# Gate and up projections of the second channel mixer as seven block products of sums

## The chip, the cores and the metric

One core of a Trainium2 chip. The metric is the device time of one execution in microseconds, the median over the runs shown. The kernel is written in Bass with Tile: the program names tiles in pools, and a scheduler at build time sets the order of every engine's queue except TensorE's, which here runs in the order of the program.

## The reference, cut to what matters

The reference is one inference step of a two-layer backbone: 512 latent tokens and 128 context tokens, 640 in all, of width 1024. After the token mixers of each layer comes a SwiGLU channel mixer with a hidden width of 2816:

```python
def ffn_sublayer(x, mods, p):
    h = modulated_norm(x, p['norm2_g'], mods[3], mods[4])
    y = (jax.nn.silu(h @ p['ffn_w_gate']) * (h @ p['ffn_w_up'])) @ p['ffn_w_down']
    return x + mods[5] * y
```

All of it is in float32. The two projections `h @ ffn_w_gate` and `h @ ffn_w_up` of layer 1 (the second and last layer) are what the change rewrites.

## The kernel before, in words

The kernel keeps features on the partitions and the 640 tokens along the free axis. A float32 product runs on TensorE as three passes of the type float32r: each operand is split into a high part (a copy into float32r, on ScalarE, line 308) and a low part (source minus high part, on VectorE, line 309; both in `split`), and the passes are high by high, high by low, low by high. A pass over one 128 by 128 block of weights is a weight load and a matmul (`mm`, line 351).

The channel mixer stands in `run` (line 2070 and on). The hidden width is cut into 22 tiles of 128 features (index `f`), in three parts of 8, 7 and 7 tiles (`THIRDS`). For each tile, `fm_tile` loads a 128 by 1024 block of gate weights into a staging buffer (`weights`, tag `wst`, three buffers, one DMA of 512 KB on SyncE's queue, line 315), splits it into the tags `whi` and `wlo` (two buffers each), and runs 8 blocks of the contraction times 3 passes times 2 token halves: 48 matmuls, of 256 and of 384 columns (`SPLIT`). The same follows for the up weights. ScalarE takes the SiLU of the gate out of PSUM (line 2120), VectorE multiplies it by the up result (line 2128), and the product is split again (lines 308 and 309) into a tile `g` (tag `g`, 12 buffers). After a part, eight tiles of down weights (index `e`) multiply the part's `g` tiles, and `residual` (line 1810) adds the result to `x`. In the last part the down products run one token half after the other, so that the final norm can start early, and some of their split weights lie in buffers that `spare` finds.

Layer 1's first tiles differ: the gate and up of tile 0 and the gate of tile 1 run together by token halves (`by_halves`), because the normalised tokens `h` of the second half are still being made then (`norm_k`, whose low parts of odd blocks are made on GpSimd, line 584). `h` holds high and low parts of all 8 blocks of the width for 640 tokens. Nothing reads `h` after the last up projection of layer 1.

The accumulators are five PSUM banks handed out in turn. Nothing but the scheduler orders ScalarE, VectorE, GpSimd and the DMA queue among each other; a tile of a tag gets one of that tag's buffers when one is free, and its first writer waits until all readers of the buffer's last tile are done.

Of the kernel before, what the change touches and what calls it, by code (L numbers as in the profile page):

```python
# [11 lines left out]
F32 = mybir.dt.float32  # L12
F32R = mybir.dt.float32r
I32 = mybir.dt.int32
AF = mybir.ActivationFunctionType
ALU = mybir.AluOpType
# [4 lines left out]
D = 1024  # L21
KD = 8
NS = 512
NP = 128
T = NS + NP
HB = 256
SPLIT = (slice(0, HB), slice(HB, T))
L = 2
PAST = 256
FF = 2816  # L30
KF = FF // 128
# [256 lines left out]
class _Build:  # L288
# [35 lines left out]
    @staticmethod  # L324
    def spare(e, l, pool, n):

        tile = lambda shape, tag, bufs: pool.tile(shape, F32R, tag=tag, name="w2", bufs=bufs)
        if e < 2:
            ts = [tile([128, 2, T], "g", 12) for _ in range(2)]
        elif e == 3:  # L330
            t = tile([128, 2, D], "cb", 1)
            ts = [t[:, i] for i in range(2)]
        elif e in (4, 5):
            ts = [tile([128, D], *(("wmd", 2) if e == 4 else ("sg", 3))) for _ in range(2)]
        else:
            return None
        ts = [t.rearrange("p a n -> p (a n)") if len(t.shape) == 3 else t for t in ts]
        return [t[:, 0:128 * n].rearrange("p (k n) -> p k n", k=n) for t in ts]

    def put(self, oh, k, a, src, view=None):  # L340
# [334 lines left out]
    def half_steps(self, w, rhs, ks, h, acc, tag="fd"):  # L675

        od = self.od
        yield tag, 1
        o = self.half_tile(acc, tag, h)
        n = len(ks)  # L680
        for i, k in enumerate(ks):
            for c, (wt, part) in enumerate(((w[0], 0), (w[0], 1), (w[1], 0))):
                self.mm(o, wt[:, i, :], rhs(part, k)[:, SPLIT[h]], i == 0 and c == 0, i == n - 1 and c == 2)
            yield od.now
        return o

    def tm_chunk(self, srcs, h, n, pools, sink, room=None):

# [1381 lines left out]
    def run(self):  # L2070
        nc, A = self.nc, self.A
# [9 lines left out]
        h = hp.tile([128, 2, KD, T], F32R, tag="h", name="h", bufs=1)  # L2081
# [6 lines left out]
        ps = self.banks(P, W)  # L2088
        for l in range(L):
            hp, h, h_st, x, fx, fx_st, P, W = self.mixer(l, h, h_st, x, fx, fx_st, P, W, p_side, w_side)  # L2090
            p_side, w_side = w_side, p_side
            ps = self.banks(P, W)
            gpool, g_st = self.pool("g", side="left")
            for part, (f0, f1) in enumerate(THIRDS):
                g, kept = {}, {}
                last = lambda e, n=f1 - f0: self.weights(A["wd"][l, e, :, f0:f1], [128, n, 128],
                                                         parts=self.spare(e, l, gpool, n))
                for f in range(f0, f1):
                    if f == KF - 1:
                        kept.update((e, last(e)) for e in (0, 1))  # L2100
                    if f == 0:
                        r = []
                        parts = [gpool.tile([128, 2, T], F32R, tag="g", name="w2", bufs=12).rearrange("p a t -> p (a t)")
                                 [:, 0:D].rearrange("p (k n) -> p k n", k=KD) for _ in range(2)]
                        gen = self.by_halves([A["wg"][l, f], A["wu"][l, f]], lambda q, k, h=h: h[:, q, k], ps,
                                             more=(A["wg"][l, 1], parts))
# [8 lines left out]
                        og = og1  # L2115
                    else:
                        og = self.fm_tile(A["wg"][l, f], lambda q, k: h[:, q, k], range(KD), ps)
                    sg = gpool.tile([128, D], F32, tag="sg", name="sg", bufs=3)[:, :T]
                    for q in range(2):
                        nc.scalar.activation(sg[:, SPLIT[q]], og[q], AF.Silu)  # L2120
                    if f:
                        ou = self.fm_tile(A["wu"][l, f], lambda q, k: h[:, q, k], range(KD), ps)
                    if l + 1 < L:
                        self.modulate(f, gpool)
                    g[f - f0] = gt = gpool.tile([128, 2, T], F32R, tag="g", name="g", bufs=12)
                    for q in range(2):
                        s = SPLIT[q]
                        nc.vector.tensor_tensor(out=sg[:, s], in0=ou[q], in1=sg[:, s], op=ALU.mult)  # L2128
# [81 lines left out]
```

## Time and profile before

| | |
|---|---|
| three runs | 1956.04, 1961.34, 1962.57 us (median 1961.34) |
| the profiled execution | 1962.85 us, of which the span in the profile is 1961.0 us |
| mean granted TensorE clock | 0.978 of full speed |

The span runs from the first to the last instruction; the 1.85 us around it belong to the execution as well. In the rows further down times are microseconds from the start of the span, and a group of instructions is given by source line, engine, operation and the tiles it writes and reads. PE is TensorE's matmuls, PEld its weight loads (which overlap the matmuls), DVE is VectorE, ACT ScalarE, POOL GpSimd. A matmul's duration in these rows includes its way through the array; how many follow each other per microsecond is read from their start times.

### The profile page before, as it was taken

To read this page: it belongs to the slowest core of one execution; us is meant where nothing else is said; L and a number is where in the kernel's file an instruction comes from. 1 tells how busy PE (TensorE), PEld (TensorE's weight loads), DVE (VectorE), ACT (ScalarE), POOL (GpSimd) and SP (SyncE) were. 2 spreads that over 40 slices of the span, in tenths; PEclk is the share of its full clock that TensorE was granted. 3 is DMA by queue.
4 is the path that set the end of the run, shared out by engine and by line. 5 is a ranking of instruction groups with operands and counts; after the bars stand their busy time and mean duration, and the time that the engine had idled before them with its cause. 6 is when DMAs were issued, how large, how long until landed. Compare 5 with 4: busy or idle time off the path is not lost.

```text
span 1961.0 us, 40272 instructions
## 1 busy us (share of the span) xinstructions
PE 1847.3 (94%) x16620; PEld 1742.0 (89%) x16620; DVE 1070.1 (55%) x2304; ACT 727.5 (37%) x1497; POOL 329.7 (17%) x530
## 2 busy tenths in 40 slices
PE   5998998899999999999999999789999999999997
PEld 4986787778999999999998988678889999999997
DVE  6573546677557547647555854567655232233244
ACT  4632124766442112222346322367645221221231
POOL 1221521233300000000133271123322000000001
PEclk9997899999999999999999999899999999999999
DMA  7345423142445436436423322213342222222221
GB/s 299 122 119 135 125 78 104 31 110 79 139 138 172 140 108 193 150 109 189 133 91 101 98 66 67 77 44 84 95 151 65 76 76 76 76 68 83 75 97 54
DMA packets 114166, 210.35 MB, mean 107 GB/s; under 512 B 44160, under 2 KB 61312, under 8 KB 113856
## 3 DMA queue, kind: packets, MB, share of 16 engines
q1 hardware_dynamic: 105920, 202.74, 32.8%
q0 software_dynamic: 2816, 4.72, 1.2%
q8 instruction: 130, 2.13, 0.4%
q10 hardware_dynamic: 5248, 0.33, 0.2%
q14 instruction: 52, 0.43, 0.1%
HBM read 183.14 MB, written 19.89 MB: 104 GB/s over the span
## 4 chain that ended last, share of the span: by engine, by line
PE 78%; DVE 9%; ACT 5%; DMA 5%; issue 2%; POOL 1%; SPq 0%; DVEq 0%; ACTq 0%; POOLq 0%
PE acc L351 56%; PE tacc L351 6%; PE pvo L351 2%; PE ptp L363 2%; PE sc L351 2%; PE mpart L351 1%; PE invp L351 1%; DMA wst<-wout 1%; DVE wlo L309 1%; ACT p L1294 1%; ACT whi L308 1%; DMA wmd<-wmodT 1%; DMA wmd<-wmod 1%; ACT pt L1329 1%; PE ysp L351 1%
## 5 line engine op out<-in xcount | busy, mean ns | idle before, releaser
L351 PE MATMUL acc<-h,whi 128*128 128x256 f32 (+1 forms) x3520 | 679.0, 312 | 3.2 <-ACT h L574 1.4
L351 PEld LDWEIGHTS acc<-h,whi 128*128 128x128 f32 x3520 | 578.5, 189 | 11.7 <-issue 3.4
L308 ACT CAST whi<-wst 128x1024 fp32r<-128x1024 f32 (+3 forms) x202 | 196.9, 976 | 687.9 <-PE acc L351 645.0
L351 PE MATMUL acc<-h,wlo 128*128 128x256 f32 (+1 forms) x1760 | 411.1, 310 | 0.8 <-DVE wlo L309 0.8
L309 DVE TENSOR_TENSOR wlo<-wst,whi 128x1024 fp32r<-128x1024 f32 (+3 forms) x202 | 229.9, 1139 | 204.2 <-ACT whi L308 199.3
L351 PEld LDWEIGHTS acc<-h,wlo 128*128 128x128 f32 x1760 | 320.4, 189 | 2.5 <-DVE wlo L309 1.3
L351 PE MATMUL acc<-g,whi 128*128 128x256 f32 (+1 forms) x1128 | 216.7, 309 | 0.1
L541 POOL TENSOR_TENSOR sq<-sq 128x256 f32<-128x256 f32 (+1 forms) x48 | 45.4, 947 | 927.2 <-ACT sq L535 926.9
L1810 DVE SCALAR_TENSOR_TENSOR x<-acc,mods,x 128x256 f32<-128x256 f32 (+1 forms) x192 | 75.3, 434 | 210.6 <-PE acc L351 210.4
L351 PEld LDWEIGHTS acc<-g,whi 128*128 128x128 f32 x1128 | 185.9, 188 | 0.4 <-DVE g L309 0.4
L507 DVE SCALAR_TENSOR_TENSOR wmj<-wmd,cb 128x1024 f32<-128x1024 f32 x112 | 136.8, 1222 | 40.9 <-DMA wmd<-wmodT 39.6
L351 PE MATMUL tacc<-whi,h 128*128 128x256 f32 (+1 forms) x640 | 151.2, 317 | 1.0 <-ACT whi L308 0.8
L351 PE MATMUL acc<-g,wlo 128*128 128x384 f32 (+1 forms) x564 | 135.2, 309 | 0.0
L351 PEld LDWEIGHTS tacc<-whi,h 128*128 128x128 f32 x640 | 111.4, 194 | 11.8 <-issue 6.6
L351 PE MATMUL acc<-oh,whi 128*128 128x384 f32 (+1 forms) x512 | 114.6, 314 | 3.3 <-DVE xe L1810 1.9
L363 PE MATMUL ptp<-cbase,p 128*128 128x128 f32 x512 | 80.3, 283 | 27.8 <-ACT pt L1329 14.1
L351 PEld LDWEIGHTS acc<-g,wlo 128*128 128x128 f32 x564 | 103.2, 188 | 0.0
L351 PE MATMUL tacc<-wlo,h 128*128 128x256 f32 (+1 forms) x320 | 98.2, 307 | 1.3 <-DVE wlo L309 1.3
L363 PEld LDWEIGHTS ptp<-cbase,p 128*128 128x128 f32 x512 | 56.6, 141 | 43.9 <-ACT pt L1329 17.6
L2128 DVE TENSOR_TENSOR sg<-acc,sg 128x256 f32<-128x256 f32 x88 | 39.2, 485 | 101.9 <-PE acc L351 101.9
L1297 POOL TENSOR_SCALAR dg<-cbase,sd 128x128 f32<-128x128 f32 x96 | 58.8, 613 | 207.1 <-DVE sd L1295 150.0
L1294 ACT ACTIVATE p<-sc,sm 128x768 f32<-128x768 f32 (+1 forms) x96 | 79.8, 831 | 31.8 <-DVE sm L1291 23.6
(321 smaller groups left out, 2655.9 us busy)
## 6 DMA issues: line engine op xcount, KB each, us to landing
wmd<-wmodT SPq DMA_DIRECT2D x56, 512.0 KB
wst<-wg SPq DMA_DIRECT2D x44, 512.0 KB
wst<-wu SPq DMA_DIRECT2D x44, 512.0 KB
wmd<-wmod SPq DMA_DIRECT2D x40, 512.0 KB
wst<-wd SPq DMA_DIRECT2D x34, 448.0 KB
wst<-wfm SPq DMA_DIRECT2D x24, 512.0 KB
wst<-wd SPq DMA_DIRECT2D x16, 512.0 KB
wst<-wtma SPq DMA_DIRECT2D x12, 512.0 KB
```

What stands on the lines that cost most here:

```text
L308: self.nc.scalar.copy(hi, src)
L309: self.nc.vector.tensor_tensor(out=lo, in0=src, in1=hi.bitcast(F32), op=ALU.subtract)
L351: self.nc.tensor.matmul(out, lhsT, rhs, start=start, stop=stop)
L363: self.nc.tensor.transpose(out, in_, self.ident)
L507: nc.vector.scalar_tensor_tensor(out=j, in0=st, scalar=1.0, in1=self.cb[:, g], op0=ALU.mult, op1=ALU.mult, accum_out=self.msum[:, e, g:g + 1])
L541: (eng or nc.gpsimd).tensor_tensor(out=self.sq[hf][0], in0=self.sq[hf][0], in1=sq, op=ALU.add)
L1294: nc.scalar.activation(p, s, AF.Exp, bias=m, accum_out=d)
L1297: nc.gpsimd.tensor_scalar(out=dg, in0=self.ident, scalar1=d, scalar2=None, op0=ALU.mult)
L1329: nc.scalar.copy(pt[:, a:a + m].rearrange("p a b -> p (a b)"), tp[:, :128 * m])
L1810: self.nc.vector.scalar_tensor_tensor(out=x_out[:, a:b], in0=o[h][:, a - HB * h:b - HB * h], scalar=m[:, 8 * gate + e, grp:grp + 1], in1=x ...
L2128: nc.vector.tensor_tensor(out=sg[:, s], in0=ou[q], in1=sg[:, s], op=ALU.mult)
```

## The change

From tile 3 on, in layer 1 only (`by_sums`), the gate and up products of a tile are taken as one product of a 2 by 2 block matrix with a 2 by 2 block matrix: the rows of the first are gate and up, its columns the two halves of the contraction (4 blocks of 128 each); the second has the two halves of the contraction by the left and right 320 tokens (`HT`). The seven products of the Winograd form of Strassen's scheme replace the eight block products. Each is 4 blocks times 3 passes: 12 matmuls of 320 columns (`product`).

`sums_of_tokens` runs once, at tile 3: GpSimd rebuilds the tokens from their parts (8 additions), VectorE makes the four sums t1 to t4 of blocks (8 subtractions of 640 elements), and they are split (8 times a ScalarE copy and a VectorE subtraction of 640 elements); three go to a new tile `tt`, and t1 over the right half of `h`.

`seven` runs for each of the 19 tiles 3 to 21. The two weight loads stay (staging now has a fourth buffer, tag `wsx`). GpSimd makes the sums s1, s3, s2 and s4 of weight blocks in place in the staging buffers, and two of the seven low parts (of a22 and a12). The other five low parts are on VectorE, all seven high parts on ScalarE; each split is of 512 elements in place of 1024. The split weights lie in six buffers: two each of the tags `whi`, `wlo` and a new `sw`, taken in turn, each holding high and low parts of one 128 by 512 block. The products are summed by one ScalarE copy and seven VectorE additions of 320 elements from PSUM into `sg` and `up`, with two SiLUs of 320 elements. Then `up` is multiplied by `sg` and split into `g`, as before. The spare places of the last part's down weights change with it (`room`), and `g` has 9 buffers in place of 12 in layer 1.

```diff
@@ -25,6 +25,7 @@
 HB = 256
 SPLIT = (slice(0, HB), slice(HB, T))
+HT = T // 2
...
+    def room(self, e, l, pool, n):
+        if e == 0:
+            ts = [pool.tile([128, KD, 128], F32R, tag="sw", name="w2", bufs=2) for _ in range(2)]
+        elif e == 1:
+            ts = [pool.tile([128, 2, T], F32R, tag="g", name="w2", bufs=self.gbufs) for _ in range(2)]
+        elif e == 3:
+            t = self.left_room = pool.tile([128, 3, 2, 4, HT], F32R, tag="tt", name="w2", bufs=1)
+        if e in (3, 4, 5):
+            t = self.left_room.rearrange("p a b c d -> p (a b c d)")
+            ts = [t[:, 128 * n * i:128 * n * (i + 1)] for i in (2 * e - 6, 2 * e - 5)]
+        elif e > 1:
+            return None
+        ts = [t.rearrange("p a b -> p (a b)") if len(t.shape) == 3 else t for t in ts]
...
+    def sums_of_tokens(self, h, pool):
+        nc = self.nc
+        left, right = slice(0, HT), slice(HT, T)
+        raw = [pool.tile([128, 2, T], F32, tag="g", name="hraw", bufs=self.gbufs) for _ in range(4)]
+        for hf in range(2):
+            for p in range(4):
+                v = [h[:, q, 2 * p:2 * p + 2, SPLIT[hf]] for q in range(2)]
+                nc.gpsimd.tensor_tensor(out=raw[p][:, :, SPLIT[hf]], in0=v[0].bitcast(F32), in1=v[1].bitcast(F32),
+                                        op=ALU.add)
+        tt = pool.tile([128, 3, 2, 4, HT], F32R, tag="tt", name="tt", bufs=1)
+        v = nc.vector.tensor_tensor
+        for p in range(2):
+            b11, b12 = raw[p][:, :, left], raw[p][:, :, right]
+            b21, b22 = raw[p + 2][:, :, left], raw[p + 2][:, :, right]
+            v(out=b11, in0=b12, in1=b11, op=ALU.subtract)
+            v(out=b12, in0=b22, in1=b12, op=ALU.subtract)
+            v(out=b22, in0=b22, in1=b11, op=ALU.subtract)
+            v(out=b21, in0=b21, in1=b22, op=ALU.subtract)
+            for i, t in enumerate((b22, b12, b21)):
+                self.split(*[tt[:, i, q, 2 * p:2 * p + 2] for q in range(2)], t)
+        for p in range(2):
+            self.split(*[h[:, q, 2 * p:2 * p + 2, right] for q in range(2)], raw[p][:, :, left])
+        b = lambda q, k, s: h[:, q, 4 * k:4 * k + 4, s]
+        self.tokens = {
+            "b11": [b(q, 0, left) for q in range(2)], "t1": [b(q, 0, right) for q in range(2)],
+            "b21": [b(q, 1, left) for q in range(2)], "b22": [b(q, 1, right) for q in range(2)],
+        }
+        for i, n in enumerate(("t2", "t3", "t4")):
+            self.tokens[n] = [tt[:, i, q] for q in range(2)]
+    def seven(self, srcs, acc, pool):
+        nc = self.nc
+        raw = []
+        for src in srcs:
+            self.raws += 1
+            r = (pool.tile([128, KD, 128], F32, tag="wsx", name="wst", bufs=1) if self.raws % 4 == 3 else
+                 self.wp.tile([128, KD, 128], F32, tag="wst", name="wst", bufs=3))
+            nc.sync.dma_start(out=r, in_=src)
+            raw += [r[:, 0:4], r[:, 4:8]]
+        a11, a12, a21, a22 = raw
+        def slot():
+            i = self.slots = (self.slots + 1) % 3
+            p, tag = ((self.wp, "whi"), (self.wp, "wlo"), (pool, "sw"))[i]
+            t = p.tile([128, KD, 128], F32R, tag=tag, name="sw", bufs=2)
+            return t[:, 0:4], t[:, 4:8]
+        g, v = nc.gpsimd.tensor_tensor, nc.vector.tensor_tensor
+        w = {}
+        w["a11"], w["s2"], w["a12"], w["s3"], w["s1"], w["a22"] = [slot() for _ in range(6)]
+        def by_pool(hi, lo, src):
+            nc.scalar.copy(hi, src)
+            g(out=lo, in0=src, in1=hi.bitcast(F32), op=ALU.subtract)
+        self.split(*w["a11"], a11)
+        by_pool(*w["a22"], a22)
+        g(out=a22, in0=a21, in1=a22, op=ALU.add)
+        g(out=a21, in0=a11, in1=a21, op=ALU.subtract)
+        g(out=a11, in0=a22, in1=a11, op=ALU.subtract)
+        self.split(*w["s2"], a11)
+        by_pool(*w["a12"], a12)
+        g(out=a12, in0=a12, in1=a11, op=ALU.subtract)
+        self.split(*w["s3"], a21)
+        self.split(*w["s1"], a22)
+        def product(a, b):
+            o = acc.tile([128, 512], F32, tag="w", name="acc")[:, 0:HT]
+            wt, tok = w[a], self.tokens[b]
+            for k in range(4):
+                for c, (i, j) in enumerate(((0, 0), (0, 1), (1, 0))):
+                    self.mm(o, wt[i][:, k], tok[j][:, k], k == 0 and c == 0, k == 3 and c == 2)
+            return o
+        sg = pool.tile([128, T], F32, tag="sg", name="sg", bufs=3)
+        up = pool.tile([128, T], F32, tag="sg", name="up", bufs=3)
+        c11, c12, c21, c22 = sg[:, 0:HT], sg[:, HT:], up[:, 0:HT], up[:, HT:]
+        p1 = product("a11", "b11")
+        w["s4"] = slot()
+        self.split(*w["s4"], a12)
+        p6 = product("s2", "t2")
+        nc.scalar.copy(c11, p1)
+        v(out=c12, in0=p6, in1=c11, op=ALU.add)
+        p2 = product("a12", "b21")
+        v(out=c11, in0=p2, in1=c11, op=ALU.add)
+        nc.scalar.activation(c11, c11, AF.Silu)
+        p7 = product("s3", "t3")
+        v(out=c21, in0=p7, in1=c12, op=ALU.add)
+        p5 = product("s1", "t1")
+        v(out=c22, in0=p5, in1=c21, op=ALU.add)
+        v(out=c12, in0=p5, in1=c12, op=ALU.add)
+        p4 = product("a22", "t4")
+        v(out=c21, in0=p4, in1=c21, op=ALU.add)
+        p3 = product("s4", "b22")
+        v(out=c12, in0=p3, in1=c12, op=ALU.add)
+        nc.scalar.activation(c12, c12, AF.Silu)
+        return sg, up
 
...
@@ -2091,16 +2213,34 @@
             p_side, w_side = w_side, p_side
             ps = self.banks(P, W)
             gpool, g_st = self.pool("g", side="left")
+            by_sums = l == L - 1
+            plain = 3 if by_sums else KF
+            self.gbufs = 9 if by_sums else 12
+            self.slots = self.raws = -1
             for part, (f0, f1) in enumerate(THIRDS):
                 g, kept = {}, {}
                 last = lambda e, n=f1 - f0: self.weights(A["wd"][l, e, :, f0:f1], [128, n, 128],
-                                                         parts=self.spare(e, l, gpool, n))
+                                                         parts=(self.room if by_sums else self.spare)(e, l, gpool, n))
                 for f in range(f0, f1):
+                    if f >= plain:
+                        if f == plain:
+                            self.sums_of_tokens(h, gpool)
+                        sg, up = self.seven([A["wg"][l, f], A["wu"][l, f]], ps, gpool)
+                        g[f - f0] = gt = gpool.tile([128, 2, T], F32R, tag="g", name="g", bufs=self.gbufs)
+                        if f < KF - 1:
+                            nc.vector.tensor_tensor(out=up, in0=up, in1=sg, op=ALU.mult)
+                            self.split(gt[:, 0], gt[:, 1], up)
+                            continue
+                        for s in (slice(0, HT), slice(HT, T)):
+                            nc.vector.tensor_tensor(out=up[:, s], in0=up[:, s], in1=sg[:, s], op=ALU.mult)
+                            self.split(gt[:, 0, s], gt[:, 1, s], up[:, s])
+                        kept.update((e, last(e)) for e in (0, 1))
+                        continue
                     if f == KF - 1:
                         kept.update((e, last(e)) for e in (0, 1))
                     if f == 0:
                         r = []
-                        parts = [gpool.tile([128, 2, T], F32R, tag="g", name="w2", bufs=12).rearrange("p a t -> p (a t)")
+                        parts = [gpool.tile([128, 2, T], F32R, tag="g", name="w2", bufs=self.gbufs).rearrange("p a t -> p (a t)")
                                  [:, 0:D].rearrange("p (k n) -> p k n", k=KD) for _ in range(2)]
                         gen = self.by_halves([A["wg"][l, f], A["wu"][l, f]], lambda q, k, h=h: h[:, q, k], ps,
                                              more=(A["wg"][l, 1], parts))
@@ -2115,14 +2255,14 @@
                         og = og1
                     else:
                         og = self.fm_tile(A["wg"][l, f], lambda q, k: h[:, q, k], range(KD), ps)
-                    sg = gpool.tile([128, D], F32, tag="sg", name="sg", bufs=3)[:, :T]
+                    sg = gpool.tile([128, T if by_sums else D], F32, tag="sg", name="sg", bufs=3)[:, :T]
                     for q in range(2):
                         nc.scalar.activation(sg[:, SPLIT[q]], og[q], AF.Silu)
                     if f:
                         ou = self.fm_tile(A["wu"][l, f], lambda q, k: h[:, q, k], range(KD), ps)
                     if l + 1 < L:
                         self.modulate(f, gpool)
-                    g[f - f0] = gt = gpool.tile([128, 2, T], F32R, tag="g", name="g", bufs=12)
+                    g[f - f0] = gt = gpool.tile([128, 2, T], F32R, tag="g", name="g", bufs=self.gbufs)
                     for q in range(2):
                         s = SPLIT[q]
                         nc.vector.tensor_tensor(out=sg[:, s], in0=ou[q], in1=sg[:, s], op=ALU.mult)
```

## Rows read from the trace of the kernel before

**Rows 1.** The page's busy times: engine, us busy (share of the span), instructions.

```profile
span 1961.0 us, 40272 instructions
PE 1847.3 (94%) x16620; PEld 1742.0 (89%) x16620; DVE 1070.1 (55%) x2304; ACT 727.5 (37%) x1497; POOL 329.7 (17%) x530
```

**Rows 2.** The page's chain that ended last, by engine and by line.

```profile
PE 78%; DVE 9%; ACT 5%; DMA 5%; issue 2%; POOL 1%; SPq 0%; DVEq 0%; ACTq 0%; POOLq 0%
PE acc L351 56%; PE tacc L351 6%; PE pvo L351 2%; PE ptp L363 2%; PE sc L351 2%; PE mpart L351 1%; PE invp L351 1%; DMA wst<-wout 1%; DVE wlo L309 1%; ACT p L1294 1%; ACT whi L308 1%; DMA wmd<-wmodT 1%; DMA wmd<-wmod 1%; ACT pt L1329 1%; PE
```

**Rows 3.** Busy by stretch: length, PE, PEld, DVE, ACT, POOL, clock, DMA share, GB/s.

```profile
1497.00:1525.00 28.00, 27.59 (x181) 27.10 (x180) 7.63 (x9) 7.07 (x12) 1.02 (x1) 1.00 0.25 76
1553.00:1595.00 42.00, 42.00 (x290) 42.00 (x289) 12.23 (x15) 10.47 (x16) 0.00 (x0) 1.00 0.25 76
```

**Rows 4.** ACT in order of time: start, us, what; layer 1, tiles 3, 4.

```profile
1524.87 1.05 ACT L308 CAST whi<-wst 128x1024 fp32r<-128x1024 f32 x1 [5.25 <-PE acc L351]
...
1552.87 1.05 ACT L308 CAST whi<-wst 128x1024 fp32r<-128x1024 f32 x1 [5.25 <-PE acc L351]
```

**Rows 5.** Groups by shape, 1480 to 1961: count | busy, mean ns | idle.

```profile
L351 PE MATMUL acc<-h,whi 128*128 128x384 f32 x688 | 214.2, 336 | 0.0
L309 DVE TENSOR_TENSOR g<-sg,g 128x640 fp32r<-128x640 f32 x21 | 17.2, 819 | 0.0
L308 ACT CAST g<-sg 128x640 fp32r<-128x640 f32 x21 | 15.3, 730 | 1.4 <-DVE sg L2128 0.3
L2128 DVE TENSOR_TENSOR sg<-acc,sg 128x384 f32<-128x384 f32 x22 | 12.1, 548 | 0.0
L2120 ACT ACTIVATE sg<-acc 128x384 f32<-128x384 f32 x22 | 10.6, 484 | 0.0
L2128 DVE TENSOR_TENSOR sg<-acc,sg 128x256 f32<-128x256 f32 x22 | 9.3, 424 | 96.5 <-PE acc L351 96.5
L2120 ACT ACTIVATE sg<-acc 128x256 f32<-128x256 f32 x22 | 8.3, 376 | 4.1 <-PE acc L351 4.1
L309 DVE TENSOR_TENSOR g<-sg,g 128x384 fp32r<-128x384 f32 x1 | 0.6, 553 | 0.0
L308 ACT CAST g<-sg 128x384 fp32r<-128x384 f32 x1 | 0.5, 510 | 0.0
```

**Rows 6.** POOL in order of time, the norm ahead of the stage.

```profile
1455.02 1.40 POOL L541 TENSOR_TENSOR sq<-sq 128x256 f32<-128x256 f32 x1 [2.01 <-ACT sq L535]
...
1460.27 0.74 POOL L541 TENSOR_TENSOR sq<-sq 128x256 f32<-128x256 f32 x1 [0.76 <-ACT sq L535]
1465.54 1.00 POOL L541 TENSOR_TENSOR sq<-sq 128x384 f32<-128x384 f32 x1 [4.53 <-ACT sq L535]
...
1490.88 1.02 POOL L584 TENSOR_TENSOR h<-nt,h 128x384 fp32r<-128x384 f32 x1 [10.81 <-ACT nt L578]
...
1497.08 1.02 POOL L584 TENSOR_TENSOR h<-nt,h 128x384 fp32r<-128x384 f32 x1 [1.17 <-ACT nt L578]
```

**Rows 7.** Line 966 on POOL over the span: ns min/median/max of one.

```profile
L966 POOL TENSOR_TENSOR decay<-cbase,fg x10: 1038/1365/2020, 94.6 to 1077.6; 128x512 f32<-128x512 f32 x10
```

**Rows 8.** All engines in order of time, 1502 to 1505, the hops between engines.

```profile
1502.08 1.05 ACT L308 CAST whi<-wst 128x1024 fp32r<-128x1024 f32 x1 [5.07 <-PE acc L351]
...
1503.16 1.23 DVE L309 TENSOR_TENSOR wlo<-wst,whi 128x1024 fp32r<-128x1024 f32 x1 [6.70 <-ACT whi L308]
...
1504.44 0.56 PE L351 MATMUL acc<-h,wlo 128*128 128x256 f32 x2 [0.41 <-DVE wlo L309]
```

**Rows 9.** DVE in order of time at 1454, beside the first of rows 6.

```profile
1454.59 1.23 DVE L309 TENSOR_TENSOR wlo<-wst,whi 128x1024 fp32r<-128x1024 f32 x1 [1.34 <-ACT whi L308]
```

**Rows 10.** POOL, then DVE, in order of time at 94 to 98.

```profile
94.59 4.76 POOL L966 TENSOR_TENSOR decay<-cbase,fg 128x512 f32<-128x512 f32 x3
...
96.72 1.73 DVE L309 TENSOR_TENSOR wlo<-wst,whi 128x1024 fp32r<-128x1024 f32 x1
```

More of the change, by code (lines that the diff above doesn't have):

```diff
@@ L337, in spare @@
         ts = [t.rearrange("p a n -> p (a n)") if len(t.shape) == 3 else t for t in ts]
+        return [t[:, 0:128 * n].rearrange("p (k n) -> p k n", k=n) for t in ts]
+    def room(self, e, l, pool, n):
[11 more added lines that the diff above has]
+        ts = [t.rearrange("p a b -> p (a b)") if len(t.shape) == 3 else t for t in ts]
         return [t[:, 0:128 * n].rearrange("p (k n) -> p k n", k=n) for t in ts]
```

## The prediction

> **What bounds the kernel now.** I read the page's busy times first [rows 1]: TensorE 94% of the span, VectorE 55%, ScalarE 37%, GpSimd 17%. The chain that ended last says the same [rows 2]: 78% of it is TensorE, most on the accumulators of the large projections. [...] The price of a tile is a period: the same split comes back at 1524.87 and, two tiles later, at 1552.87, which is 14.00 us per tile [rows 4]. A tile has 96 matmuls and 30,720 columns.
>
> **Part 1, fewer matmuls.** A tile becomes 7 x 12 = 84 matmuls of 320 columns, 26,880 columns. Matmuls and columns both fall to 7/8, so whatever share of the pace is fixed per instruction, the tile takes 12.25 us if nothing stalls it, and a product takes U = 1.75 us. That is 1.75 us per tile, and 19 tiles give 33.25 us, the most that the change can bring.
>
> **Part 2, load on the other engines.** A 512-element operation lies between rows: on ScalarE 0.51 us for 384 and 0.73 for 640, so 0.62; on VectorE with both inputs in SBUF 0.553 and 0.819, so 0.69; an addition of 320 from PSUM 0.49, ScalarE from PSUM 0.43 [rows 5]. On GpSimd an undisturbed operation takes 0.74 us for 256 and 1.00 for 384 [rows 6]; carried on, 1.27 for 512. Its only 512-element rows run from 1.04, with broadcast operands, to a median of 1.365 [rows 7]; I keep 1.27 and these as ends. Per tile: ScalarE 7 x 0.62 + 3 x 0.43 + 0.73 = 6.4 us; VectorE 5 x 0.69 + 7 x 0.49 + 2 x 0.82 = 8.5; GpSimd 6 x 1.27 = 7.6. None reaches 12.25, so no engine bounds the tile by its sum. The DMA bytes stay the same, staging has four buffers, and a load issued when the buffer of two tiles back is free has most of a tile to land; I cost it at nothing.
>
> **Part 3, the chain of sums.** This decides. GpSimd works in place, so its queue is one strict chain: low part of a22, then s1 over a22, s3 over a21, s2 over a11. Only then can s2 be split, and its product p6 is the second of the tile. The chain cannot begin before the split of a22 has a buffer. There are two per tag, a22 comes ahead of a12 in the program, and the two that its tag frees next are those of the preceding tile's s3 (read last by p7, the fourth product) and s4 (p3, the seventh). If buffers go out in the order of first use, a22 gets s3's. Then from the end of p7 until p6 of the next tile TensorE has p5, p4, p3 and p1: 4 x 1.75 = 7.00 us of cover. Against it stand: 0.16 until p7's last result is out (a matmul's 336 ns [rows 5] less its turn of some 0.175), ScalarE's high part 0.62, four GpSimd operations 5.08, ScalarE's high part of s2 0.62, VectorE's low part 0.69, four hops of 0.05 (0.03 and 0.05 in [rows 8]) 0.20, less two matmuls (0.29) that run before the first low part is wanted: 7.08 us. Cover and chain are equal within 0.1 us; any wait inside the chain is lost on TensorE, in each of 16 passages from tile to tile (4 + 6 + 6). The first tile of each part is free of it, since seven or more microseconds of other matmuls precede it.
>
> **Part 4, waits inside the chain.** GpSimd and VectorE disturb each other. A GpSimd addition of 256 that began at 1455.02 took 1.40 us in place of 0.74 [rows 6]: VectorE was in a subtraction with both inputs in SBUF until 1455.82 [rows 9], and the addition ended 0.60 after that. The other way round, VectorE's 1.23 us became 1.73 beside a run of GpSimd additions [rows 10]. So one meeting costs GpSimd up to 0.69 - 0.14 = 0.55 and VectorE from 0.5 to a whole GpSimd operation. Of VectorE's seven such operations per tile I expect one in the chain's 5 us (the low part of s3, whose buffer comes free after p5): 0.5. The low part of s2 then meets GpSimd's next operation, a12's low part, which starts as soon as s2 is done: 0.6, half of 1.27. The stall is 0.08 + 1.1 = 1.2 us, and the tile 13.45. The bounds are no meeting (stall 0 to 0.1; 0 with GpSimd at 1.04, whose chain is 0.9 shorter; 0.4 at 1.365) and every GpSimd operation meeting one, 4 x 0.5 + 1.1 (stall 3.2, tile 15.4).
>
> [...]
>
> **Part 5, queues and the start.** Behind the waiting split of a22 on ScalarE stand copies and SiLUs of the current tile; five PSUM banks let TensorE go on for four products, so a short wait there costs nothing by itself. On GpSimd only the tile's other five operations stand behind it, on TensorE everything behind p6. The sums of tokens: GpSimd 4 x 1.27 + 4 x 1.9 = 12.7 us, four of them in its 10.8 us idle before 1490.88, the others among the low parts of `h` until 1497.08 [rows 6], which they can hold up by 1.9 us each; TensorE takes a block of that half in about 1.6 us, later than GpSimd makes it, so 0 to 2 us. VectorE's 8 x 0.82 + 8 x 0.82 = 13.1 us beside the 7.63 it already has in the 28 us to 1525 [rows 3] fit. I take 1 us. The end of the last part, with other spare buffers, I cost at nothing: eight tiles of down products cover the splits.
>
> **The sum.** 3 x 1.75 + 16 x (14.00 - 13.45) - 1 = 5.25 + 8.8 - 1 = 13 us gained. The profiled execution of 1962.85 us (span 1961.0, 1.85 around it) becomes 1949.8; it stands 1.5 over the median, so the median goes from 1961.3 to **1948**.
>
> **The rivals.** *The cover holds*: GpSimd a little quicker than 1.27, or a queue order without meetings. Stall 0 to 0.1, gain 30 to 32, time 1930. For it: the unmet chain is as long as the cover. Against it: seven VectorE operations of the disturbing kind per tile. [...] *The buffer of a22 is that of s4*, handed out in the order of the calls: the chain begins at the end of p3, only p1 covers it, the tile takes 10.5 + 7.1 = 17.6 or more, 5.25 - 57.6 - 1 = -53, time 2014. The trace shows nothing of it; first use is where a tile needs its memory, so it has little.
>
> **How the numbers follow.** What a measurement here tells from no change is about 0.3%, 6 us. Forecast 0.50 (own range 1941 to 1956; 0.44 faster, 0.06 same), cover 0.22 (faster), interface 0.22 (0.07 same, 0.15 slower), buffer 0.06 (slower). Faster 0.66, same 0.13, slower 0.21. The range 1930 to 1972 leaves out the last rival, the heavy end of the interface (0.08) and the light end of the cover (0.06).
>
> **What would show it.** Right: the period of a tile between 12.9 and 13.9 us; TensorE idle once per tile, ahead of the product of s2, ended by its low part on VectorE or its high part on ScalarE; GpSimd operations of 512 near 1.27, some stretched to 1.7; 84 matmuls per tile at 0.146 us. Wrong: a period of 12.3 (cover), 14.3 or more with most GpSimd operations stretched (interface), 17 with GpSimd beginning only at the end of p3 (buffer), or TensorE's idle time ahead of another product or at the start of the stage.

## The result, and the profile after

The changed kernel takes **2035.36 us** (median of 4 runs, 2030.41 to 2039.17) against 1961.95 beside it on the same chip: a ratio of 1.0378, interval 1.0346 to 1.0411. The forecast was 1948, with 1930 to 1972 as its range; the kernel is slower by 73 us where a gain of 13 was expected. The profiled execution has a span of 2037.4 us.

The page's busy times and its chain, in the order of [rows 1, 2]:

```profile
span 2037.4 us, 40486 instructions
...
PE 1861.5 (91%) x16392; PEld 1747.2 (86%) x16392; DVE 1207.8 (59%) x2492; ACT 780.9 (38%) x1619; POOL 509.2 (25%) x652
...
PE 74%; DVE 13%; DMA 6%; ACT 4%; issue 2%; SPq 1%; POOL 0%; DVEq 0%; ACTq 0%; POOLq 0%
PE acc L368 52%; PE tacc L368 6%; PE pvo L368 3%; PE ptp L380 2%; PE sc L368 2%; DVE sw L310 2%; DVE up L2231 1%; PE invp L368 1%; DMA wst<-wout 1%; DMA wmd<-wmod 1%; DVE wlo L310 1%; PE mpart L368 1%; ACT p L1416 1%; ACT whi L309 1%; DMA w
```

The 228 matmuls are gone (16,620 to 16,392), yet TensorE is busy 14 us longer, and there are 76 us more of span. VectorE's low parts (L310 `sw`) and its multiply (L2231) are new in the chain. The idle time has one main place, as TensorE's waits from 1520 us on show (line waited for: us in total, times, longest):

```profile
PE acc L368 <- DVE sw L310: 44.2, 16, 2.8
PE acc L368 <- ACT tt L309: 14.8, 1, 14.8
...
PE acc L368 <- DVE tt L310: 3.0, 2, 1.5
```

Sixteen waits of up to 2.8 us are the sixteen passages from tile to tile. In the kernel before, TensorE's only waits after 1525 us are 4.0 us in the final norm. One passage, all engines in order of time (start, us, what; L764 is the low part of a22 or a12 on GpSimd, L768, L769, L770 and L773 are s1, s3, s2 and s4):

```profile
1576.05 1.93 PE L368 MATMUL acc<-h,sw 128*128 128x320 f32 x12
1576.24 0.62 ACT L763 CAST sw<-wst 128x512 fp32r<-128x512 f32 x1 [0.76 <-PE acc L368]
...
1576.94 1.29 POOL L764 TENSOR_TENSOR sw<-wst,sw 128x512 fp32r<-128x512 f32 x1 [8.13 <-ACT sw L763]
...
1578.31 1.30 POOL L768 TENSOR_TENSOR wst<-wst 128x512 f32<-128x512 f32 x1
...
1579.69 1.28 POOL L769 TENSOR_TENSOR wst<-wst 128x512 f32<-128x512 f32 x1
...
1581.05 1.30 POOL L770 TENSOR_TENSOR wst<-wst 128x512 f32<-128x512 f32 x1
...
1582.31 1.73 POOL L764 TENSOR_TENSOR sw<-wst,sw 128x512 fp32r<-128x512 f32 x1
...
1582.82 1.90 DVE L2231 TENSOR_TENSOR up<-up,sg 128x640 f32<-128x640 f32 x1
...
1583.15 0.56 PE L368 MATMUL acc<-tt,sw 128*128 128x320 f32 x2
...
1584.12 1.73 POOL L773 TENSOR_TENSOR wst<-wst 128x512 f32<-128x512 f32 x1
1584.64 2.35 DVE L310 TENSOR_TENSOR sw<-wst,sw 128x512 fp32r<-128x512 f32 x2
...
1586.45 1.87 PE L368 MATMUL acc<-tt,sw 128*128 128x320 f32 x10 [2.74 <-DVE sw L310]
...
1588.11 3.36 PE L368 MATMUL acc<-h,sw 128*128 128x320 f32 x12
...
1593.97 1.30 POOL L764 TENSOR_TENSOR sw<-wst,sw 128x512 fp32r<-128x512 f32 x1 [8.12 <-ACT sw L763]
```

Product p7 ends as p5's matmuls begin (1576.05); the split of a22 starts 0.19 us later. The four GpSimd operations run undisturbed at 1.28 to 1.30 us, and s2 is ready at 1582.35, nearly as planned. Then VectorE is late. Its multiply has been queued ahead of the low part of s2, and takes 1.90 us instead of 0.82, because GpSimd works on a12's low part until 1584.0 and the two engines hold each other up (GpSimd's operation takes 1.73 us there, against 1.29 at 1576.94). The low part of s2 starts at 1584.64 beside s4, and TensorE may go on only at 1586.45. From one L764 to the next of its kind is 17.03 us.

The 2.74 us of idling don't fill the difference to 12.3. TensorE's twelve matmuls at 1588.11 take 3.36 us in place of the 1.93 at 1576.05, which the windows explain (columns as in [rows 3]):

```profile
1559.89:1576.94 17.05, 14.23 (x86) 13.83 (x85) 10.42 (x14) 5.92 (x11) 8.61 (x6) 0.90 0.21 63
...
1587.00:1588.00 1.00, 1.00 (x9) 1.00 (x8) 1.00 (x2) 0.00 (x0) 0.00 (x0) 0.94 0.00 0
1588.00:1589.00 1.00, 1.00 (x6) 1.00 (x5) 0.82 (x2) 0.62 (x1) 0.00 (x0) 0.50 0.71 188
1589.00:1590.00 1.00, 1.00 (x6) 1.00 (x5) 0.69 (x1) 0.00 (x0) 0.00 (x0) 0.50 0.87 340
1590.00:1591.00 1.00, 1.00 (x5) 1.00 (x5) 0.00 (x0) 0.00 (x0) 0.00 (x0) 0.50 0.81 250
1591.00:1592.00 1.00, 1.00 (x7) 1.00 (x7) 0.49 (x1) 0.00 (x0) 0.00 (x0) 0.86 0.60 229
...
1527.00:1545.00 18.00, 4.89 (x34) 4.62 (x32) 14.77 (x12) 4.89 (x8) 15.06 (x9) 0.77 0.18 58
1545.00:1560.00 15.00, 10.31 (x44) 9.38 (x45) 10.43 (x16) 5.33 (x8) 0.11 (x1) 0.59 0.00 1
```

After the stall the granted clock stands at 0.50 for three microseconds. What is missing to 1.00 in these five rows adds up to 0.06 + 3 x 0.50 + 0.14 = 1.70 us. What it costs is a little less: in the run without the multiply, further down, passages with and without the fall have the same waits, and differ by 1.53 us. Interruptions have a price beside their idle time, too. The two matmuls ahead of the stall show 0.56 us where at full pace they take a turn of 0.147 each, 0.27 us too much; the first of them starts 0.05 late; and the first one after the stall takes 0.41 us in place of 0.31, another 0.10. 12.32 of work + 2.74 + 0.42 + 1.53 = 17.01 us: the tile. Sixteen passages cost 16 x (17.05 - 14.00) = 49 us.

The last two of these rows are the stage's start, where TensorE is busy 4.89 of 18 us. GpSimd in order of time, the end of the norm (L601 answers to the last of [rows 6]) and the start of the stage:

```profile
1502.29 1.02 POOL L601 TENSOR_TENSOR h<-nt,h 128x384 fp32r<-128x384 f32 x1 [1.16 <-ACT nt L595]
1516.23 2.56 POOL L764 TENSOR_TENSOR sw<-wst,sw 128x512 fp32r<-128x512 f32 x2 [12.92 <-ACT sw L763]
...
1527.02 15.04 POOL L717 TENSOR_TENSOR hraw<-h 128x512 f32<-128x512 f32 x8
```

The tokens are complete at 1503.3, but the additions that rebuild them (L717) are queued behind the weight sums of tile 3, and start at 1527.02. TensorE waits 14.8 + 3.0 us for what is made of them, and then works at 0.59.

The sum against the span: the sixteen passages 49 us, the first tile with sums 20, the down products at the end 6 (from the last product by sums to the end 70.2 us, before 64.4: TensorE waits 1.8 + 0.7 us there for split weights, and then works at 0.50 from 1972 to 1976), the first tiles of the two other parts 3.5 less; 71.5 worked out so, 71.4 by the trace (1529.97 to 2037.4 against 1525.0 to 1961.0, from the first matmul of tile 3). The other 5 us arise upstream, ahead of the stage (the norm's last low part begins at 1502.29 instead of 1497.08). They are not the change's work: up to 1470 us TensorE, ScalarE, VectorE and GpSimd do the same instructions in the same order in all ten traces of this document. That upstream part still differs between these traces by some 17 us from end to end, and 17 executions of the kernel before alone spread from 1955.4 to 1968.4 us. So beside each time I give the **stage**: from the start of that low part to the end of the span, 1961.0 - 1497.1 = 463.9 us before, 2037.4 - 1502.3 = 535.1 after. Each is read from one execution.

### The profile page after: what moved, and what is told of

Same layout as the page of the kernel before. It is cut to its first block, busy times and chain, and to the rows that moved or that the text cites. A ratio compares the mean times of both kernels' runs of the same rounds, so it can differ in the third digit from the quotient of the medians.

```text
span 2037.4 us, 40486 instructions
## 1 busy us (share of the span) xinstructions
PE 1861.5 (91%) x16392; PEld 1747.2 (86%) x16392; DVE 1207.8 (59%) x2492; ACT 780.9 (38%) x1619; POOL 509.2 (25%) x652
## 3 DMA queue, kind: packets, MB, share of 16 engines
q1 hardware_dynamic: 105920, 202.74, 31.5%
## 4 chain that ended last, share of the span: by engine, by line
PE 74%; DVE 13%; DMA 6%; ACT 4%; issue 2%; SPq 1%; POOL 0%; DVEq 0%; ACTq 0%; POOLq 0%
PE acc L368 52%; PE tacc L368 6%; PE pvo L368 3%; PE ptp L380 2%; PE sc L368 2%; DVE sw L310 2%; DVE up L2231 1%; PE invp L368 1%; DMA wst<-wout 1%; DMA wmd<-wmod 1%; DVE wlo L310 1%; PE mpart L368 1%; ACT p L1416 1%; ACT whi L309 1%; DMA wmd<-wmodT 1%
## 5 line engine op out<-in xcount | busy, mean ns | idle before, releaser
L368 PE MATMUL acc<-h,whi 128*128 128x256 f32 (+1 forms) x2304 | 453.8, 315 | 2.5 <-ACT h L591 1.4
L368 PEld LDWEIGHTS acc<-h,whi 128*128 128x128 f32 x2304 | 380.9, 190 | 11.3 <-issue 3.7
L368 PE MATMUL acc<-h,wlo 128*128 128x256 f32 (+1 forms) x1152 | 274.1, 313 | 0.8 <-DVE wlo L310 0.8
L310 DVE TENSOR_TENSOR wlo<-wst,whi 128x1024 fp32r<-128x1024 f32 (+3 forms) x164 | 185.7, 1134 | 108.0 <-ACT whi L309 107.5
L368 PEld LDWEIGHTS acc<-h,wlo 128*128 128x128 f32 x1152 | 211.2, 190 | 2.5 <-DVE wlo L310 1.3
L368 PE MATMUL acc<-tt,sw 128*128 128x320 f32 x684 | 122.7, 326 | 62.0 <-DVE sw L310 44.2
L368 PEld LDWEIGHTS acc<-tt,sw 128*128 128x128 f32 x684 | 106.5, 195 | 69.8 <-DVE sw L310 48.4
L368 PE MATMUL acc<-h,sw 128*128 128x320 f32 x912 | 165.5, 340 | 0.0
L368 PEld LDWEIGHTS acc<-h,sw 128*128 128x128 f32 x912 | 160.0, 218 | 0.0
L764 POOL TENSOR_TENSOR sw<-wst,sw 128x512 fp32r<-128x512 f32 x38 | 56.6, 1492 | 263.7 <-ACT sw L763 263.7
L309 ACT CAST sw<-wst 128x512 fp32r<-128x512 f32 x95 | 56.8, 616 | 133.6 <-POOL wst L769 70.5
```

What stands on the lines that cost most here:

```text
L309: self.nc.scalar.copy(hi, src)
L310: self.nc.vector.tensor_tensor(out=lo, in0=src, in1=hi.bitcast(F32), op=ALU.subtract)
L368: self.nc.tensor.matmul(out, lhsT, rhs, start=start, stop=stop)
L764: g(out=lo, in0=src, in1=hi.bitcast(F32), op=ALU.subtract)
```

## The experiments

The theory: VectorE's queue and its meetings with GpSimd (*queue and port* in the expectations: each holds the other up, here 1.90 us in place of 0.82 and 1.73 in place of 1.29) make the low part of s2 late, the stall costs the clock, and the start is a matter of queue order. The kernels with one run below stand beside one run of 1971.6 us of the kernel before (the first four) or its median of 1962.24. The rivals: GpSimd is too slow as such; the work of the two engines adds up and bounds the tile whatever the order; the slow matmuls have nothing to do with the stall.

**Token additions earlier.** The additions are called at tile 1, the rest stays at tile 3.

```diff
+                    if f == 1 and by_sums:
+                        self.sums_of_tokens(h, gpool)
...
-                            self.sums_of_tokens(h, gpool)
+                            self.sums_of_raw(h, gpool)
```

> The eight GpSimd additions that rebuild the tokens are called two tiles earlier in the program (tile 1 in place of tile 3); everything else is as changed. Theory: the 17.8 us that TensorE waits in the first tile by sums (14.8 + 1.5 + 1.5) come from these additions starting only at 1527 us, behind the weight sums of that tile, with GpSimd idle for 12.9 us before. Then the wait falls to 0 to 3 us and the time by 15 to 20 us, to about 2015 to 2020; the tiles after it keep their period of 17.0 us. Rival: the additions wait for something else than their place in the program (a buffer); then they start as late and the time stays at 2035.

Measured: 2027.18 us (one run), stage 520.0, 15 us less than after. The additions begin at 1506.36, and TensorE's waits in the stage are now:

```profile
PE acc L368 <- DVE sw L310: 49.4, 17, 5.0
...
PE acc L368 <- ACT sw L309: 2.2, 1, 2.2
```

The wait of 14.8 us is gone; waits of 5.0 and 2.2 us remain in tile 3, for weight parts instead of token parts, more than the 0 to 3 that were expected, and the total is above the 2015 to 2020 as well. So most of the start was queue order, worth 15 of the 20 us; tiles later on keep their period (17.03 us).

**Without the multiply.** The multiply of `up` by the SiLU is left out.

```diff
-                            nc.vector.tensor_tensor(out=up, in0=up, in1=sg, op=ALU.mult)
```

> Leaves out the multiplication of up by the SiLU of the gate in the tiles by sums, all but the last (up alone goes into g). Theory, queue and port: the low part of s2 is late because it stands on VectorE behind that multiplication, which GpSimd holds up (1.90 us in place of 0.82), and is then itself held up; without the multiplication the stall of 2.74 us per tile falls to 0.5 to 1.5 and the period from 17.0 to between 13 and 15 us (time 1985 to 2010, the late start unchanged). Rival, chain: GpSimd's four operations are simply too long for the cover; then the stall stays above 2 us and the period near 17. Rival on the clock: the granted clock falls for some 3.5 us in each tile because TensorE has stood still; if a shorter stall leaves it at 1.00, the tile gains another 1.8 us.

Measured: 1992.31 us (one run), stage 501.6. TensorE's waits:

```profile
PE acc L368 <- DVE sw L310: 16.3, 16, 1.0
...
PE acc L368 <- ACT sw L309: 7.9, 16, 0.5
```

Each passage has 1.0 + 0.5 us of waiting in place of 2.74, and the period is 14.37 us (L764 at 1561.06 and 1575.44). With two interruptions, 12.32 + 1.51 + 2 x 0.27 = 14.37: in this passage nothing is left for the clock. It isn't so in all, although the waits are the same in all 16 (0.49 or 0.50, and 1.01 or 1.02): the product after the stall takes 1.92 or 1.93 us in 10 of the 16 passages and 2.68 to 3.09 in the other 6 (in the changed kernel 3.08 to 3.37 in all 16). Two of them in TensorE's order of time:

```profile
1585.39 1.92 PE L368 MATMUL acc<-h,sw 128*128 128x320 f32 x12
...
1600.36 2.85 PE L368 MATMUL acc<-h,sw 128*128 128x320 f32 x12
```

A passage of the slow kind takes 15.90 us, 1.53 more than the others. One 0.82 us operation, stretched to 1.90 and standing ahead in the queue, is worth 2.7 us of period where the clock stays, over half of that through the clock.

**Low part of s2 on GpSimd.** The two engines swap the low parts of s2 and a12.

```diff
-        self.split(*w["s2"], a11)
-        by_pool(*w["a12"], a12)
+        by_pool(*w["s2"], a11)
+        self.split(*w["a12"], a12)
```

> The low part of s2 is made on GpSimd, the low part of a12 on VectorE (swapped); nothing is left out. Queue and port: s2's low part no longer stands behind VectorE's multiplication; it comes 0.7 (ScalarE) + 1.3 (GpSimd) + 0 to 0.6 us after s2, so the stall is 0.7 to 1.4 us in place of 2.74, the period 13.5 to 15.5 and the time 1985 to 2015. Chain: one more operation on the strict chain, so the stall grows by about 0.6 and the time is 2045 or more.

Measured: 2043.03 us (one run), stage 547.1: outside the first range, and close to the numbers of the chain. All engines in order of time, one passage:

```profile
1576.51 1.72 POOL L773 TENSOR_TENSOR wst<-wst 128x512 f32<-128x512 f32 x1 [1.29 <-DVE sw L310]
...
1578.19 1.71 POOL L764 TENSOR_TENSOR sw<-wst,sw 128x512 fp32r<-128x512 f32 x1
...
1579.95 3.04 PE L368 MATMUL acc<-tt,sw 128*128 128x320 f32 x10 [3.38 <-POOL sw L764]
```

s2 is done at 1575.2, but the scheduler put s4 (L773) ahead of its low part, and s4 waited 1.29 us for VectorE to read a12. So the low part begins at 1578.19, 2.2 us after its high part is done (1575.96): here, too, the order in the queue brings the delay, and not one more operation on the chain. The stall grew to 3.38 us and the period to 17.5 to 18.9. The run doesn't tell whether GpSimd could make the part in time with s4 behind it.

**s2 in a tile of its own.** The strict chain is cut: s2 no longer needs a22's split and s1 to be done.

```diff
-        by_pool(*w["a22"], a22)
-        g(out=a22, in0=a21, in1=a22, op=ALU.add)
-        g(out=a21, in0=a11, in1=a21, op=ALU.subtract)
-        g(out=a11, in0=a22, in1=a11, op=ALU.subtract)
-        self.split(*w["s2"], a11)
+        g(out=a11, in0=a11, in1=a21, op=ALU.subtract)
+        s2 = pool.tile([128, 4, 128], F32, tag="s2", name="s2", bufs=1)
+        g(out=s2, in0=a22, in1=a11, op=ALU.subtract)
+        self.split(*w["s2"], s2)
+        g(out=a21, in0=a21, in1=a22, op=ALU.add)
         by_pool(*w["a12"], a12)
-        g(out=a12, in0=a12, in1=a11, op=ALU.subtract)
+        g(out=a12, in0=a12, in1=s2, op=ALU.subtract)
+        by_pool(*w["a22"], a22)
...
```

> The sums are rearranged so that the chain before s2 does not need a22's split: s3 = a11 - a21 in a11's place, s2 = a22 - s3 into a tile of its own (one buffer), s1 = a21 + a22 in a21's place, then the low parts of a12 and a22 and s4. Both theories: the passage from tile to tile has no strict chain any more, the stall goes to 0 to 0.3, the period to 12.3 if TensorE bounds it; if GpSimd's operations and VectorE's two-input operations exclude each other and add up (6 x 1.30 + 5 x 0.69 + 2 x 0.82 = 12.9), 12.9 or a little more. Time 1960 to 1975, the late start unchanged. If the period stays at 15 or more, the place of the splits in the queues decides and not the chain.

Measured: 1961.41 us (one run), stage 462.0. One tile, by windows:

```profile
1593.08:1605.40 12.32, 12.32 (x86) 12.32 (x85) 9.74 (x15) 6.45 (x11) 8.86 (x6) 1.00 0.26 82
```

The same tile, all engines in order of time (L767 is now s3):

```profile
1593.08 1.29 POOL L767 TENSOR_TENSOR wst<-wst 128x512 f32<-128x512 f32 x1 [3.38 <-DVE sw L310]
...
1596.43 1.12 DVE L310 TENSOR_TENSOR sw<-s,sw 128x512 fp32r<-128x512 f32 x1 [0.77 <-ACT sw L309]
```

TensorE is busy throughout at a clock of 1.00, although the same six GpSimd operations and the same VectorE operations are done, and stretched in the same way (s2's low part takes 1.12 us in place of 0.69, and GpSimd's operation beside it 1.74 in place of 1.29). GpSimd even idles 3.38 us ahead of this tile's first sum. So neither GpSimd's speed nor the meetings bound the tile. If no two of these operations ran at the same time, a tile would take at least 6 x 1.29 + 5 x 0.69 + 2 x 0.82 = 12.8 us, an estimate from the durations here. The trace doesn't bear that sum out: a meeting with a 0.69 us operation lengthened GpSimd's 1.29 to 1.74, by 0.45, and the tile ran in 12.32.

The start remains: TensorE still waits 17.0 + 3.0 us at tile 3, which eats what the tiles gain.

**Both, and the first half of the tokens still earlier.** First the own tile together with the early additions; then also the additions of the first half of the tokens inside tile 0.

> The two edits of e1 and e4 together: the tokens' additions called at tile 1, and s2 in a tile of its own. Theory: the change loses its gain in two places only, the start (some 20 us) and the 16 passages; with both mended the stage costs 19 x 1.7 = 32 us less than before, less 5 to 12 us that the first tile by sums still waits (e1 kept two waits of 5.0 and 2.2 us there), so 20 to 27 us under the kernel before, ratio 0.986 to 0.990. Rival: the first tile's sums of weights and of tokens meet on GpSimd and VectorE, and the early additions only move the wait; then 0.993 or more.

```diff
+                        def first_hook():
+                            r.append(self.rstd(1, fx))
+                            if by_sums:
+                                self.sums_of_tokens(h, gpool, (0,))
...
-                        og, ou, og1 = self.hooked(gen, {8: lambda: r.append(self.rstd(1, fx)), 16: second})
+                        og, ou, og1 = self.hooked(gen, {8: first_hook, 16: second})
```

> As e5, and the four additions over the first token half are called while that half alone is ready (inside tile 0), when GpSimd stands idle for 10.8 us. Theory: the sums of weights of the first tile start some 5 us earlier and its waits shrink to 0 to 3 us; 3 to 6 us faster than e5. Rival: the additions hold up GpSimd's low parts of h, on which TensorE waits; then it is no faster than e5 and the wait shows at tile 0.

Measured: the first 1947.54 us (12 runs), ratio to the kernel before 0.9931, interval 0.9908 to 0.9954, stage 448.4; the second **1943.81** (6 runs), ratio 0.9912, interval 0.9891 to 0.9934, stage 442.9. Both are faster than the kernel before by their intervals, by less than 1%; the first falls short of the 0.986 to 0.990 that was expected, and stands where the rival had it (0.993 or more). Between the two the intervals overlap, so the 3.7 us that part them are not clear of noise. The tile 3 waits of 5.9 + 0.6 us in the first are gone in the second, whose waits in the stage, beside the final norm's, are mainly:

```profile
PE acc L368 <- DVE wlo L310: 3.8, 1, 3.8
PE acc L368 <- ACT w L309: 2.9, 1, 2.9
PE acc L368 <- DVE w L310: 1.6, 2, 1.3
```

Nineteen tiles at 12.34 gain 31.5 us, of which 21 reach the end of the stage. The 3.8 us stand in tile 1, where the kernel before waits 0.41 [rows 8], so part of the wait has moved there: TensorE wants a low part of weights, which VectorE begins at 1503.69, after four token sums, the first of them held by GpSimd's additions (2.46 in place of 0.82). The other waits stand at the down products of the end, and why those splits come late was not tried.

**Multiply behind s2's low part.** The changed kernel with one order pinned on VectorE: the multiply of a tile, and the split of its product, go behind the next tile's s2 split; the last tile of each part keeps its order.

```diff
+        self.pending()
...
-                        if f < KF - 1:
-                            nc.vector.tensor_tensor(out=up, in0=up, in1=sg, op=ALU.mult)
+                        def multiply(up=up, sg=sg, gt=gt):
+                            self.in_turn(nc.vector.tensor_tensor(out=up, in0=up, in1=sg, op=ALU.mult))
...
```

> The changed kernel with one change of order on VectorE: the multiplication of up by the gate is queued behind the low part of the next tile's s2 (nothing is left out, the chain and the late start stay). Queue and port: s2's low part then starts when its high part is there and waits for one GpSimd operation at most, so the stall falls from 2.74 to 0.4 to 1.1 us; with so short a stall the granted clock stays at 1.00, as in e2, and the period falls from 17.05 to 12.8 to 13.6 us: time 1975 to 1990. If only the clock's part is wrong: 14.5 to 15.5 and 2005 to 2020. Chain: the stall stays over 2 us.

Measured: 1980.32 us (one run), stage 485.9, 49 less than after. All engines in order of time, one passage:

```profile
1569.16 1.24 DVE L310 TENSOR_TENSOR sw<-wst,sw 128x512 fp32r<-128x512 f32 x1
1569.82 1.72 POOL L764 TENSOR_TENSOR sw<-wst,sw 128x512 fp32r<-128x512 f32 x1
1570.57 1.52 DVE L310 TENSOR_TENSOR sw<-wst,sw 128x512 fp32r<-128x512 f32 x1 [0.16 <-ACT sw L309]
...
1572.14 1.73 PE L368 MATMUL acc<-tt,sw 128*128 128x320 f32 x10 [1.00 <-DVE sw L310]
```

The same kernel by windows:

```profile
1560.00:1600.00 40.00, 36.53 (x240) 34.98 (x239) 28.29 (x41) 16.60 (x33) 23.83 (x17) 1.00 0.26 79
```

This kernel still does all the work, and the result is nearly that of leaving the multiply out: period 14.20 us, waits 0.34 + 1.00 (the first passage of each part has the second alone), clock 1.00. The product after the stall takes 1.92 or 1.93 us in all 16 passages, which is most of why this kernel beats the one with less work. The total is within what was expected, the waits and so the period (12.8 to 13.6) are above it: the low part of s3 (1.24) and that of s2 (1.52, both against 0.69 undisturbed) are still each held by GpSimd, and s2's high part comes 0.34 late. The multiply's place is the cause of half the stall; 1.34 us are left, of the chain and of these two low parts that GpSimd holds up.

**More work in the stall.** The changed kernel, with p1's twelve matmuls run twice.

```diff
-        def product(a, b):
+        def product(a, b, times=1):
...
-            for k in range(4):
+            for k in [0, 1, 2, 3] * times:
...
-        p1 = product("a11", "b11")
+        p1 = product("a11", "b11", 2)
```

> The changed kernel, with one edit that only adds work: the twelve matmuls of the first product of every tile (a11 by b11) run twice into the same accumulator, the second run starting the sum afresh, so the values stay the same. They stand directly ahead of the product of s2, where TensorE idles 2.74 us, and take 1.76 us. Theory (the 17.05 us of a tile are 12.32 of work, 2.74 of stall and some 2 us that the granted clock gives away because of the stall): with the stall cut to about 1.0 us by filling it, the clock stays at 1.00, the period is 12.32 + 2.74 + 0 to 0.6 = 15.1 to 15.7 us, and the kernel becomes faster by 16 times 1.35 to 1.95 less 3 times 1.76 for the first tiles of the parts: 16 to 26 us, 2009 to 2020 us in all, though TensorE does 228 matmuls more. Rival (the time after the stall is not the clock's answer to idling, but comes with the weight loads or buffers that follow, or the clock falls whatever TensorE does there): the period stays near 17.05, the time 2035 to 2041.

Measured: 2011.63 us (4 runs), ratio to the kernel before 1.0255, interval 1.0204 to 1.0306, against 1.0378 for the change: the median is 24 us lower with 228 matmuls more. Part of that is upstream, where the norm's last low part begins at 1495.17: the stage is 2010.8 - 1495.2 = 515.6 us, so 19.5 of the 26.6 us between the two profiled executions lie in it. TensorE in order of time, one tile, and a stretch by windows:

```profile
1719.20 5.45 PE L368 MATMUL acc<-h,sw 128*128 128x320 f32 x36
1724.48 0.46 PE L368 MATMUL acc<-tt,sw 128*128 128x320 f32 x2
1726.12 1.73 PE L368 MATMUL acc<-tt,sw 128*128 128x320 f32 x10 [1.18 <-DVE sw L310]
1727.69 1.93 PE L368 MATMUL acc<-h,sw 128*128 128x320 f32 x12
...
1734.74 5.45 PE L368 MATMUL acc<-h,sw 128*128 128x320 f32 x36
```

```profile
1700.00:1740.00 40.00, 37.60 (x254) 37.08 (x254) 25.79 (x36) 15.22 (x29) 24.85 (x18) 1.00 0.18 56
```

From 1719.20 to 1734.74 is 15.54 us: 12.32 + 1.76 + 1.18 + 0.27 = 15.53. Sixteen times 17.03 - 15.54, less 2 x 1.76 for the first tiles of the two other parts, is 20 us, about what the stage gains. The product after the stall, 3.36 us in the changed kernel, takes 1.92 or 1.93 in every passage, and the clock is 1.00. The tile is the same but for what TensorE does in the stall, so the slow matmuls after it, some 1.5 us per tile, were the clock's answer to the idling.

## Why the prediction was wrong

- **Part 1 was right.** That a tile of the kernel before is TensorE's own work stands in [rows 3]. A tile without a stall takes 12.32 us (own tile), forecast 12.25; a product 1.76 against 1.75.
- **Part 2 was right, and no bound.** A 512-element GpSimd operation takes 1.29 to 1.30 us where 1.27 was taken; the loads per tile stay below the tile's time, as the run with s2 in its own tile shows.
- **Part 3 was right up to s2.** The buffer of a22 is that of the preceding tile's s3, so the rival with s4's buffer falls (its period near 17 has come about in another way). s2 is ready 6.30 us after p7; by the terms of Part 3 it was 0.16 + 0.62 + 5.08 + two hops of 0.05 = 5.96.
- **Part 4 failed, first in the size of one wait.** It took 0.6 us for the low part of s2 behind GpSimd's next operation, and 0.5 for GpSimd in the chain. The latter didn't occur. The former was some 2.6: the multiply stood ahead of it in VectorE's queue, held to 1.90 by one GpSimd operation, and then the low part itself was held by the next. Part 4 counted the meetings of the chain's own operations and never asked what else VectorE could have in its queue at that moment; the multiply of the tile just ended comes due right then. That gives a stall of 2.74 us in place of 1.2. With the multiply moved away 1.34 are left, near the 1.2, in part because errors cancel: the chain is 0.34 longer than its terms and the 0.5 is missing. For the rival *interface* (0.22) the prediction asked for a period of 14.3 or more with most GpSimd operations stretched: the period came, but all four operations of the chain ran at 1.28 to 1.30, and only the two after them at 1.73. What the word stands for no run shows; the runs show operations of both engines stretched where they meet. Such meetings made the wait, but on VectorE's side (1.90 in place of 0.82) and through the order of its queue.
- **Part 4 lacked a term: the clock.** By Part 1's 12.25 us a stall of 2.7 would make a period of 14.95; the trace has 17.05. A stall of 2.74 us is followed by three microseconds at 0.50 (the clock stands there behind each of the 16), some 1.5 us per tile and 16 x 1.5 = 24 us in all, while waits of at most 1.34 us together left it at 1.00 in every passage, and waits of 1.51 in 10 of 16. Some 0.4 us per tile more are the interruptions' own. The filled stall shows the other side: with a wait of 1.2 us in its place the clock stays at 1.00.
- **Part 5 failed on the start.** It put the token additions into GpSimd's idle time ahead of 1490.88 and took 1 us. The scheduler put them behind tile 3's weight sums, at 1527.02; the cost is 20 us, and 15 of these go by calling them earlier. "The end of the last part at nothing" was wrong by 6 us.
- **The sum** had 5.25 for the three first tiles, 8.8 for the passages and -1 for the start. By the measured terms it is 3.5 for the first tiles of two parts, -49 for the passages, -20 for tile 3, -6 for the end and -5 upstream: -76.5, the span's difference of 76.4.

Open: why the upstream part, with the same work in the same order, takes some microseconds more or less from one execution to another, and the late splits of the last down products.

## What to carry to other kernels

When a change leaves two engines that hold each other up (1.90 us in place of 0.82 here) with work in a chain of little slack, list everything that can stand in each queue at the moment the chain's link comes due, not only the chain's links. Price a stall of the matrix engine with the clock it may cost afterwards: 2.74 us of waiting became 4.71 of loss here. The cure was not fewer operations but order: cutting a false dependency of in-place sums and calling early work early turned 4% slower into 0.9% faster, with the same number of operations.

## What the runs showed of the hardware beyond what was expected

- Repeating 228 matmuls for nothing made the stage 19.5 us shorter (the median 24), because TensorE's clock stayed at 1.00 where it had stood at 0.50 for three microseconds per tile.
- Meetings of VectorE operations that read two SBUF tiles with GpSimd operations stretched operations of both: 0.82 to 1.90 and 0.69 to 1.12 or more on VectorE, 1.29 to 1.74 on GpSimd. Still a tile of 12.32 us held such work of both engines that by undisturbed durations adds up to 12.8.
- How the clock answered, passage by passage: it stayed with two waits of 1.34 us together in 13 of 13 and with one of 1.2 in 16 of 16; it fell with two of 1.51 together in 6 of 16, though these waits were the same in all, and with one of 2.74 in 16 of 16. So the length of the waiting alone doesn't settle it.
- A wait of TensorE cost some 0.27 us more than its idle time shows, once for each interruption: the last matmul ahead of it lasts 0.31 us where a turn is 0.147, and the first one after it takes 0.41 in place of 0.31. With this term three periods where the clock stayed (14.20, 14.37 and 15.54) come out within 0.01 us from the undisturbed 12.32.
